# Which gather the GpSimd queue asks for first: late V rows ahead of U rows in a four-layer decoder with product-key experts

## The chip, the core and the metric

One core of a Trainium2 chip runs the whole program as a single launch. The metric is the device time of one execution in microseconds (us). The kernel before was timed three times: 3109.57, 3111.12 and 3113.5 us, median 3111.12 us. One further execution was profiled; views, rows and windows below are of that one.

Engines are called by the profile's names: PE (matmul), DVE (vector), ACT (scalar), POOL (GpSimd), SP (sync).

## The reference, cut to what matters

A residual stream of 256 tokens by 1024 runs through four layers. Each layer is a token mixer (HGRN2, FoX, Mamba-2 SSD, HGRN2 again) and after it a PEER layer: 8 heads pick 16 experts each out of 16384 for every token, so 128 experts a token, and each expert is one row of `u_tab` and one row of `v_tab`, 1024 floats each.

```
def peer_ffn(h, w_q, sub_keys, u_tab, v_tab):
    ...
        idx = jnp.take_along_axis(cand_i, pos, axis=-1)
        gates = jax.nn.softmax(top_s, axis=-1)
        u = jnp.take(u_tab, idx, axis=0)
        v = jnp.take(v_tab, idx, axis=0)
        act = jax.nn.gelu(jnp.einsum('md,mhkd->mhk', xb, u).astype(jnp.float32), approximate=False) * gates
        return jnp.einsum('mhk,mhkd->md', act.astype(xb.dtype), v)
```

The inputs' `norm_ffn` is large, so a good part of the pre-activations is far below zero and their gelu is exactly 0; the V rows of such experts need not be read.

## The kernel before, in words

**Tiling.** A stage is one layer for one block of 128 tokens, so there are eight stages. A stage has 64 steps `i` (8 heads by 8 pairs of ranks); `i` counts on over all stages, 0 to 511. One step handles two gathers `g` = 0 and 1, each of 128 rows: 64 tokens by two ranks, one row per partition. In HBM the U row and the V row of an expert lie side by side in `uv`, 2048 floats.

**What a step does.** `dot(i, g)` on DVE multiplies the gathered U half with the tokens and adds up (one SCALAR_TENSOR_TENSOR of 128x1024, line 219, through a helper). `scaled(i, g)` on ACT takes the gelu. `spread(i)` builds diagonal matrices of the gated activations on ACT and lets PE add the V rows into the stage's sums (`add_rows`, line 1715). Between these, the mixer of the next stage and the routing of coming heads are issued in small portions, so PE, DVE and ACT do both kinds of work in one written order. `ask(i)` on DVE writes an index list for the V rows: a row whose gelu is 0 gets an index beyond the table, and the DMA skips it.

**Three kinds of gather, all issued on POOL's queue in the written order.**
- W (line 1625): a whole row, U and V, 128x2048, 1 MB. It is used for `g` = 0 of even steps.
- U (line 1625): the U half alone, 128x1024, 512 KB. It is used for `g` = 1 of every step but the last few, and also for `g` = 0 of odd steps (where `split(i)` holds).
- V (line 1643, `rest_of`): the V half that belongs to a U. It can be asked for only once `ask(i)` has run, and it skips rows.

Every one of these is one DMA_INDIRECT instruction on POOL, which is busy while it writes the descriptors; the data follow on the DMA engines. Eight completion semaphores go round (DMASW0 to DMASW7), so an issue also waits for the landing of the DMA eight issues earlier.

**Places.** The gathers land in seven buffers of 2048 floats a partition, used as whole places (W) or halves (U, V); `pool[2]` and `pool[1]` are first-in first-out lists of the free ones. `taken` pops the first; `leave` gives it back. A U half goes back when its `dot` is written (`dot`, line 1683), a V half or whole row when its sum is written (`add_rows`, line 1719). The list is filled while the program is built; on the chip the new gather waits for the last reader of its place, which is DVE for a place that a U left and PE for a place that a V or W left.

**Order around the change.** `fetches(n)` is called at the start of step `n`. It asks for the U gather of step n+2 with `g` = 1 (NH = 3), the U or W gather of step n+3 with `g` = 0 (NW = 4), and the V gathers of step n-1: one when n-1 is even, two (`g` = 1, then `g` = 0) when n-1 is odd. Before, the loop put `rest_of(n - 1)` ahead of the first gather with `g` = 0, which comes second in the list; the U gather with `g` = 1 went out ahead of it. The V rows of a step are summed later: `g` = 1 at step i+3 (LAG), `g` = 0 of odd steps at step i+4 (`behind`).

**The bound.** `bounds_check` of a V gather is an integer; each of the 730 calls loads it into a fresh POOL register first.

Of the kernel before, what the change touches and what calls it, by code (L numbers as in the profile page):

```python
# [19 lines left out]
P = 128  # L20
# [3 lines left out]
DEPTH = 4  # L24
# [10 lines left out]
STAGES = 2 * DEPTH  # L35
# [145 lines left out]
def trunk(ctx: ExitStack, tc: tile.TileContext, d: dict, out: bass.AP):  # L181
    nc = tc.nc
# [51 lines left out]
    def C(name):  # L234
        o, n = CONST[name]
        return cst[:, o:o + n]
# [5 lines left out]
    ident, weights = fst[:, 0:P], fst[:, P:]  # L242
    after = C("after")
    tri = C("rb")[:, 0:P]
    small = cpool.tile([P, 2], F32, name="eps")
    eps, spare = small[:, 0:1], small[:, 1:2]
    trimask = cpool.tile([P, P], U8, name="trimask")
# [89 lines left out]
    for l in range(DEPTH):  # L337
        k = KIND[l]
        n = UNITS[UK[k]]
# [16 lines left out]
    for l in range(DEPTH):  # L356
# [9 lines left out]
        for u in ours:  # L366
            t, _, i, where, again = kept[u]
# [1034 lines left out]

    def split(i):

        return i % 2 == 1 and 4 <= i < 64 * (STAGES - 1)

    def apart(i, g=1):

        return g == 1 and i < CLOSE or g == 0 and split(i) or i >= CLOSE + 2

    def route(s, hh):
# [89 lines left out]
        else:  # L1501
# [11 lines left out]
            for o, g, i, j in places:  # L1513
                vec.tensor_copy(gs[o, g], igv[i, :, :, j])
            n = 64 * s + 8 * hh
            halves = ([(gs[:, 0, 0, 1:NQ:2], 0)] if split(n + 1) else []) + [(gs[:, 1, 0], 0)] if n + NQ <= CLOSE else [(gs[:, 1, 0, 0:CLOSE - n], 0), (gs[:, :, 0, CLOSE + 2 - n:], 0)]
            for v, _ in halves:
                vec.tensor_scalar(v, v, 2.0, None, op0=OP.mult)
# [49 lines left out]
    asks = {}  # L1568
# [19 lines left out]
    def taken(n, key):  # L1588

        place[key] = pool[n].pop(0)  # L1590
# [24 lines left out]
    def rows(i, g):  # L1615

        if i >= CLOSE + 2:
            return at_end(4 + 2 * i - 2 * CLOSE + g)
        return place["V", i, g] if apart(i, g) else buffer(i, g)[:, D:]

    def fetch(i, g):
        s, hh, q = pairs[i]
        if i < CLOSE or i < CLOSE + 2 and not g:
            taken(1 if apart(i, g) else 2, ("U" if apart(i, g) else "W", i, g))
        nc.gpsimd.indirect_dma_start(buffer(i, g), None, halved if apart(i, g) else d["uv"],  # L1625
                                     bass.IndirectOffsetOnAxis(ap=got[s, hh][0][:, g, q:q + 1], axis=0))

    def ask(i):

        s, hh, q = pairs[i]  # L1630
        a, n = acts[i], 1 + split(i)
        g = slice(2 - n, 2)
        o = (i // 2 * 3 + i % 2) % 12
        w = index_ring[:, o:o + n]
        vec.tensor_scalar(a[:, g], a[:, 4 - n:4], 0.0, float(FAR), op0=OP.is_equal, op1=OP.mult)
        stt(w, a[:, g], 1.0, got[s, hh][1][:, g, 0, q], op0=OP.add, op1=OP.add)
        asks[i] = [(k, w[:, k + n - 2:k + n - 1]) for k in ((1, 0) if n == 2 else (1,))]

    def rest_of(i):

        for g, w in asks.pop(i):
            taken(1, ("V", i, g))
            nc.gpsimd.indirect_dma_start(rows(i, g), None, halved, bass.IndirectOffsetOnAxis(ap=w, axis=0),  # L1643
                                         bounds_check=2 * DEPTH * P * P - 1, oob_is_err=False)

    def last_rows():

        ix, gs, _ = got[STAGES - 1, 7]
        vec.tensor_scalar(ix[:, :, 0:2], gs[:, :, 0, NQ - 2:], 1.0, None, op0=OP.add)
        for k in range(2):  # L1650
            for g in range(2):
                nc.gpsimd.indirect_dma_start(rows(CLOSE + 2 + k, g), None, halved,
                                             bass.IndirectOffsetOnAxis(ap=ix[:, g, k:k + 1], axis=0))

    def known(i):

        s, hh, _ = pairs[i]
        return got[s, hh][2] if (s, hh) in got else 0

    def fetches(n):  # L1660

        while sent[0] < len(jobs_):
            i, g = jobs_[sent[0]]
            if pairs[i][2] >= known(i) or i >= n + (NH if g else NW) and n < CLOSE - 2:
                break
            if n - 1 in asks and not g:
                rest_of(n - 1)
            if i < CLOSE and not pool[1 if apart(i, g) else 2]:
                break
            fetch(i, g)  # L1670
            sent[0] += 1
        if n - 1 in asks:
            rest_of(n - 1)
        if n == CLOSE:
            last_rows()

# [174 lines left out]
    for s in range(STAGES):  # L1851
# [23 lines left out]
        for i in range(64 * s, 64 * s + 64):  # L1875
            now[0] = i
            if i == 64 * (STAGES - 1) - 3:
                for k in (1, 0):
                    give(2, mix[:, (17 + 2 * k) * D:(19 + 2 * k) * D])
            new, end = i % 64 in TWICE and s > 0, i % 64 == 63 and s + 1 < STAGES  # L1880
            fetches(i)
            dot(i, 0)
            scaled(i, 0)
# [52 lines left out]
```

## Time and profile before

| | |
|---|---|
| median of three runs | 3111.12 us |
| the profiled execution | 3082.27 us |
| its span, first to last instruction | 3080.5 us |
| mean granted PE clock | 0.924 |
| busy PE / DVE / ACT / POOL | 84% / 73% / 48% / 65% |
| moved by DMA | 1221.21 MB, 396 GB/s over the span |
| on POOL's software queue | 1025.36 MB, 83.9% of the time of 16 DMA engines |
| on SP's hardware queue (weights) | 193.55 MB, 15.3% |

The profiled execution is 1.8 us longer than its span and about 29 us (0.9%) shorter than the median of the timed runs. A change that is worked out from the trace is therefore added to the median.

Busy POOL time is time in which it writes descriptors. "Idle before, releaser" in a row is the time in which the engine stood still before that instruction, and what ended it. In a window's row, the last two columns are the mean busy share of the 16 DMA engines (a share a little over 1 comes from packets that overlap) and what they moved.

### The profile page before, as it was taken

Reading aid. Unit: us, or ns where it says so; the run is one execution under the profiler, and the core shown is the slowest. Engines: PE = TensorE matmul, PEld = TensorE weight load, DVE = VectorE, ACT = ScalarE, POOL = GpSimd, SP = SyncE. Lnnn points to the kernel's source line nnn. Section 1 sums busy time; section 2 is a strip of 40 time slices with the busy share of each in tenths; the row PEclk is TensorE's granted clock in tenths of the full one; section 3 lists DMA queues with packets and bytes.
Section 4 is the critical chain, followed back from the end, with each engine's and each line's share of the span. In section 5 each row is a group of like instructions: output and inputs, shape, how many; then the busy total and the mean of one; then the engine's idle time right before and its main releaser. Section 6 shows DMA issues by size and latency. Waiting matters only on the chain.

```text
span 3080.5 us, 36036 instructions
## 1 busy us (share of the span) xinstructions
PE 2585.2 (84%) x9490; PEld 1113.8 (36%) x9490; DVE 2263.0 (73%) x6722; ACT 1470.2 (48%) x4410; POOL 2001.7 (65%) x1766
## 2 busy tenths in 40 slices
PE   9899887988789878999788998889877898976556
PEld 4434343333225424344223543343323253342222
DVE  1687677877877857888687787678768767787764
ACT  2355344464344633687335674355534544443333
POOL 0376576766767766766576655667667676776664
PEclk9999998998899999999889999999988999987887
DMA  7699999999999999999999999999999999999998
GB/s 313 264 396 411 415 405 412 408 413 411 388 404 408 411 404 412 385 414 405 409 384 390 401 413 411 399 400 377 413 410 391 394 412 413 398 392 415 412 414 328
DMA packets 281435, 1221.21 MB, mean 396 GB/s; under 512 B 43099, under 2 KB 43739, under 8 KB 220944
## 3 DMA queue, kind: packets, MB, share of 16 engines
q0 software_dynamic: 253152, 1025.36, 83.9%
q1 hardware_dynamic: 28080, 193.55, 15.3%
q8 instruction: 78, 1.28, 0.2%
q14 instruction: 125, 1.02, 0.1%
HBM read 1266.23 MB, written 1.05 MB: 411 GB/s over the span
## 4 chain that ended last, share of the span: by engine, by line
DMA 43%; PE 23%; DVE 21%; ACT 5%; issue 5%; POOL 2%; POOLq 0%; DVEq 0%; ACTq 0%
DMA arena<-in_uv,ix 25%; DMA arena<-in_uv,ask 17%; DVE arena L219 13%; PE pj L259 11%; PE pj L1715 9%; PE ps L259 3%; ACT L232 2%; DVE cs L219 2%; ACT dots L232 1%; DVE si L219 1%; POOL arena L1625 1%; DVE sv L219 1%; POOL arena L1643 1%; DVE gs L219 1%; ACT arena L232 1%
## 5 line engine op out<-in xcount | busy, mean ns | idle before, releaser
L219 DVE SCALAR_TENSOR_TENSOR arena<-arena 128x1024 f32<-128x1024 f32 (+3 forms) x1282 | 1304.8, 1047 | 430.6 <-DMA arena<-in_uv,ix 409.6
L1625 POOL DMA_INDIRECT arena<-in_uv,ix x1024 | 1144.2, 1117 | 627.9 <-issue 210.0
L1715 PE MATMUL pj<-arena,dh 128*64 128x512 f32 x2048 | 1125.3, 678 | 440.9 <-DMA arena<-in_uv,ask 379.8
L1643 POOL DMA_INDIRECT arena<-in_uv,ask x730 | 848.3, 1162 | 428.5 <-issue 114.6
L1715 PE MATMUL pj<-arena,dg 128*64 128x512 f32 x2048 | 1106.0, 671 | 13.4 <-ACT dg L232 13.1
L232 ACT ACTIVATE dots<-dots 128x1 f32<-128x1 f32 x1024 | 202.6, 200 | 1387.5 <-DVE arena L219 1383.1
L1715 PEld LDWEIGHTS pj<-arena,dh 128*64 128x64 f32 x2048 | 261.0, 148 | 881.4 <-issue 391.7
L259 PE MATMUL pj<-arena 128*128 128x128 f32 (+1 forms) x1752 | 508.9, 439 | 5.4 <-DVE arena L219 4.6
L232 ACT ACT_TABLE_LOAD x332 | 426.0, 1283 | 6.2 <-DVE arena L219 0.8
L259 PE MATMUL pj<-raw,arena 128*128 128x512 f32 x808 | 388.0, 615 | 4.3 <-DVE arena L219 1.9
L1715 PEld LDWEIGHTS pj<-arena,dg 128*64 128x64 f32 x2048 | 265.1, 149 | 343.9 <-issue 235.3
L259 PEld LDWEIGHTS pj<-arena 128*128 128x128 f32 x1752 | 257.6, 191 | 265.4 <-issue 239.5
L259 PEld LDWEIGHTS pj<-raw,arena 128*128 128x128 f32 x808 | 144.8, 193 | 242.5 <-issue 219.2
L232 ACT ACTIVATE dots<-dots,gs 128x1 f32<-128x1 f32 x730 | 187.6, 285 | 9.3
L219 DVE TENSOR_SCALAR dots<-dots 128x1 f32<-128x1 f32 x508 | 82.8, 163 | 122.7 <-ACT dots L232 122.5
L232 ACT ACTIVATE dh<-m,dots 128x64 f32<-128x64 f32 x508 | 168.9, 333 | 4.3 <-PE pj L1715 4.3
L259 PE MATMUL ps<-arena 128*128 128x128 f32 (+6 forms) x1120 | 150.3, 288 | 14.0 <-ACT arena L1223 8.3
L259 PEld LDWEIGHTS ps<-arena 128*128 128x128 f32 (+3 forms) x1120 | 114.5, 171 | 90.4 <-issue 37.3
L232 ACT ACTIVATE dg<-dg,dots 128x64 f32<-128x64 f32 x290 | 100.9, 348 | 9.4
L232 ACT ACTIVATE dg<-m,gs 128x64 f32<-128x64 f32 x290 | 96.4, 332 | 0.0
L219 DVE SCALAR_TENSOR_TENSOR ask<-dots,gs 128x1 int32<-128x1 f32 x508 | 81.7, 161 | 17.5
L219 DVE MAX8 sv<-arena 128x8 f32<-128x128 f32 x256 | 61.3, 281 | 32.2 <-ACT arena L1239 17.3
(131 smaller groups left out, 1875.9 us busy)
## 6 DMA issues: line engine op xcount, KB each, us to landing
raw<-in_ssm SPq DMA_DIRECT2D x48, 1024.0 KB, 8.8
raw<-in_hg SPq DMA_DIRECT2D x35, 1024.0 KB, 9.0
arena<-in_wq SPq DMA_DIRECT2D x28, 1024.0 KB, 8.9
arena<-in_hg SPq DMA_DIRECT2D x27, 1024.0 KB, 13.2
arena<-in_uv,ix POOLq DMA_INDIRECT x1028, 10.7
raw<-in_fox SPq DMA_DIRECT2D x14, 1024.0 KB, 9.2
arena<-in_uv,ask POOLq DMA_INDIRECT x730, 10.2
arena<-in_fox SPq DMA_DIRECT2D x9, 1024.0 KB, 13.9
```

The costliest lines, as they stand in the source:

```text
L219: return getattr(nc.vector, name)(o, *a, **k)
L232: nc.scalar.activation(o, i, f, **k)
L259: nc.tensor.matmul(o, w, m, start=start, stop=stop)
L1625: nc.gpsimd.indirect_dma_start(buffer(i, g), None, halved if apart(i, g) else d["uv"], bass.IndirectOffsetOnAxis(ap=got[s, hh][0][:, g, q: ...
L1643: nc.gpsimd.indirect_dma_start(rows(i, g), None, halved, bass.IndirectOffsetOnAxis(ap=w, axis=0), bounds_check=2 * DEPTH * P * P - 1, oob_ ...
L1715: nc.tensor.matmul(accs[s][e][g * 64:g * 64 + 64], diags[i, g], rows(i, g)[:, e * 512:(e + 1) * 512], start=False, stop=hh == 7 and q == N ...
```

## The change

It makes three edits. `bound` is put into a POOL register once, at the start, and every V gather uses that register. In `split` the condition `i < 64 * (STAGES - 1)` becomes `i // 64 in range(7)`; STAGES is 8, so both hold for the same steps. In `fetches` the V gathers of step n-1 are asked for ahead of the loop, so ahead of the U gather of step n+2 too.

```
+    bound = nc.gpsimd.to_reg(2 * DEPTH * P * P - 1)
...
-        return i % 2 == 1 and 4 <= i < 64 * (STAGES - 1)
+        return i % 2 == 1 and 4 <= i and i // 64 in range(7)
...
             nc.gpsimd.indirect_dma_start(rows(i, g), None, halved, bass.IndirectOffsetOnAxis(ap=w, axis=0),
-                                         bounds_check=2 * DEPTH * P * P - 1, oob_is_err=False)
+                                         bounds_check=bound, oob_is_err=False)
...
     def fetches(n):
 
+        if n - 1 in asks:
+            rest_of(n - 1)
         while sent[0] < len(jobs_):
             i, g = jobs_[sent[0]]
             if pairs[i][2] >= known(i) or i >= n + (NH if g else NW) and n < CLOSE - 2:
                 break
-            if n - 1 in asks and not g:
-                rest_of(n - 1)
             if i < CLOSE and not pool[1 if apart(i, g) else 2]:
                 break
             fetch(i, g)
             sent[0] += 1
-        if n - 1 in asks:
-            rest_of(n - 1)
         if n == CLOSE:
             last_rows()
```

Since both lists of free places are first-in first-out, the V gather now also pops the place that the U gather popped before, and the U gather the next one.

POOL's queue at steps 259 and 260, in the middle of the program, before. "in_uv,ix" marks a U or W gather, "in_uv,ask" a V gather; in brackets are the semaphores that each waits for (DMASW the eight-back landing, DVE a dot or the index list, PE a sum). The first three rows are step 259 (U of 261, V of 258, W of 262), the other four step 260 (U of 262 with `g` = 1, both V of 259, U of 263 with `g` = 0).

```order
L1625 DMA arena<-in_uv,ix 128x1024 [waits DMASW4_49,DVE_49]
L1643 DMA arena<-in_uv,ask 128x1024 [waits DMASW5_49,DVE_49,PE_49]
L1625 DMA arena<-in_uv,ix 128x2048 [waits DMASW6_49,PE_49]
L1625 DMA arena<-in_uv,ix 128x1024 [waits DMASW7_49,PE_49]
L1643 DMA arena<-in_uv,ask 128x1024 [waits DMASW0_49,DVE_49]
L1643 DMA arena<-in_uv,ask 128x1024 [waits DMASW1_49]
L1625 DMA arena<-in_uv,ix 128x1024 [waits DMASW2_49,PE_49]
```

The same seven gathers on POOL's queue after the change, same steps.

```order
L1644 DMA arena<-in_uv,ask 128x1024 [waits DMASW4_49,DVE_49]
L1626 DMA arena<-in_uv,ix 128x1024 [waits DMASW5_49,PE_49]
L1626 DMA arena<-in_uv,ix 128x2048 [waits DMASW6_49,PE_49]
L1644 DMA arena<-in_uv,ask 128x1024 [waits DMASW7_49,DVE_49,PE_49]
L1644 DMA arena<-in_uv,ask 128x1024 [waits DMASW0_49]
L1626 DMA arena<-in_uv,ix 128x1024 [waits DMASW1_49]
L1626 DMA arena<-in_uv,ix 128x1024 [waits DMASW2_49,PE_49]
```

In step 259 the U moved from first to second and its wait turned from DVE to PE; the V lost its wait for PE. In step 260 the U of 262 moved from first to third, behind both V. The W and the last U of a step keep their position, and every position keeps its DMASW semaphore. The first position of a step now always holds a V, which waits for DVE's index list.

POOL's queue at the first step that has a V gather (step 1) and the next, before.

```order
L1625 DMA arena<-in_uv,ix 128x2048 [waits DMAHW7_49]
L1625 DMA arena<-in_uv,ix 128x1024
L1643 DMA arena<-in_uv,ask 128x1024 [waits DMAHW1_49,DMASW0_49,DVE_49]
L1625 DMA arena<-in_uv,ix 128x2048 [waits DMASW1_49,PE_49]
L1625 DMA arena<-in_uv,ix 128x1024 [waits DMASW2_49]
L1643 DMA arena<-in_uv,ask 128x1024 [waits DMASW3_49,DVE_49]
```

The same place after the change.

```order
L1626 DMA arena<-in_uv,ix 128x2048 [waits DMAHW7_49]
L1644 DMA arena<-in_uv,ask 128x1024 [waits DVE_49]
L1626 DMA arena<-in_uv,ix 128x1024 [waits DMAHW1_49,DMASW0_49]
L1626 DMA arena<-in_uv,ix 128x2048 [waits DMASW1_49,PE_49]
L1644 DMA arena<-in_uv,ask 128x1024 [waits DMASW2_49,DVE_49]
L1626 DMA arena<-in_uv,ix 128x1024 [waits DMASW3_49]
```

The U of step 3 stood ahead of the first V and waited for nothing; it now stands behind it. PE, DVE, ACT and SP keep the order of their instructions; only the waits on the landings of the moved gathers go to other semaphores.

More of the change, by code (lines that the diff above doesn't have):

```diff
@@ L244, in trunk @@
     tri = C("rb")[:, 0:P]
+    bound = nc.gpsimd.to_reg(2 * DEPTH * P * P - 1)
     small = cpool.tile([P, 2], F32, name="eps")
@@ L1403, in split @@
     def split(i):
-        return i % 2 == 1 and 4 <= i < 64 * (STAGES - 1)
+        return i % 2 == 1 and 4 <= i and i // 64 in range(7)
     def apart(i, g=1):
@@ L1643, in rest_of @@
             nc.gpsimd.indirect_dma_start(rows(i, g), None, halved, bass.IndirectOffsetOnAxis(ap=w, axis=0),
-                                         bounds_check=2 * DEPTH * P * P - 1, oob_is_err=False)
+                                         bounds_check=bound, oob_is_err=False)
     def last_rows():
@@ L1660, in fetches @@
     def fetches(n):
+        if n - 1 in asks:
+            rest_of(n - 1)
         while sent[0] < len(jobs_):
@@ L1665, in fetches @@
                 break
-            if n - 1 in asks and not g:
-                rest_of(n - 1)
             if i < CLOSE and not pool[1 if apart(i, g) else 2]:
@@ L1671, in fetches @@
             sent[0] += 1
-        if n - 1 in asks:
-            rest_of(n - 1)
         if n == CLOSE:
```

## The prediction

> **What bounds the kernel now.** I read the page's slices first, then the windows, then the chains of waits, then the timeline of one place. The page's span, its DMA slices (40 equal ones of 77 us) and the two groups of gathers on POOL:
>
> ```profile
> span 3080.5 us, 36036 instructions
> ...
> DMA  7699999999999999999999999999999999999998
> GB/s 313 264 396 411 415 405 412 408 413 411 388 404 408 411 404 412 385 414 405 409 384 390 401 413 411 399 400 377 413 410 391 394 412 413 398 392 415 412 414 328
> ...
> L1625 POOL DMA_INDIRECT arena<-in_uv,ix x1024 | 1144.2, 1117 | 627.9 <-issue 210.0
> ...
> L1643 POOL DMA_INDIRECT arena<-in_uv,ask x730 | 848.3, 1162 | 428.5 <-issue 114.6
> ```
>
> The DMA engines are busy nearly throughout, and in most slices they move 404 to 415 GB/s. Where the rate falls, it falls to 377 to 399: that is so in 11 of the 37 slices between the third and the last but one (396, 388, 385, 384, 390, 399, 377, 391, 394, 398, 392). I call these the thin stretches. The windows give the same in us:
>
> ```profile
> 200.00:3000.00 2800.00, 2351.49 (x8698) 1009.26 (x8696) 2119.95 (x6300) 1364.58 (x4128) 1898.21 (x1671) 0.93 1.01 404
> ...
> 300.00:400.00 100.00, 79.06 (x236) 30.27 (x238) 63.99 (x178) 40.25 (x118) 54.84 (x49) 0.86 1.02 413
> ...
> 800.00:900.00 100.00, 79.75 (x281) 30.53 (x280) 79.29 (x231) 45.45 (x148) 78.81 (x69) 0.91 1.00 391
> ...
> 1600.00:1700.00 100.00, 87.71 (x341) 37.62 (x341) 77.41 (x230) 52.02 (x155) 69.25 (x60) 0.92 1.00 389
> ```
>
> The columns are PE, PEld, DVE, ACT and POOL busy with their counts, the granted clock, the DMA share and GB/s. A full window moves 413 GB/s at share 1.02. From 200 to 3000 us the mean is 404, so 2800 x (1 - 404/413) = 61 us is all that a better order of the same bytes could win there. The change moves no bytes. The Trainium skill has another ceiling: "DMA: Bandwidth & Descriptors", section Specifications, gives a core about 358 GB/s from HBM; by it the kernel would already be over its bound and no order could win anything. The trace disagrees with 413 GB/s in a window, so the ceiling here is the row's.
>
> What makes a stretch thin? In 800:900 POOL writes descriptors for 78.81 us in 69 gathers, and the timeline below shows 0.30 us idle ahead of each even when nothing is waited for: 78.81 + 69 x 0.30 = 99.5 of 100 us. There the issuing itself is the bound. In 300:400 it is 54.84 + 49 x 0.30 = 69.5, and POOL waits for landings. So the kernel alternates: full stretches, where DMA paces everything, and thin ones, where POOL issues back to back or waits for DVE or PE. The waits, first of DVE and PE for gathers, then of POOL:
>
> ```profile
> DVE arena L219 <- DMA arena<-in_uv,ix: 409.6, 237, 6.8
> PE pj L1715 <- DMA arena<-in_uv,ask: 379.8, 172, 8.7
> ```
> ```profile
> POOL arena L1625 <- DMA arena<-in_uv,ix: 153.1, 154, 3.8
> ...
> POOL arena L1643 <- DMA arena<-in_uv,ix: 106.7, 92, 3.1
> POOL arena L1643 <- DMA arena<-in_uv,ask: 54.1, 117, 2.3
> POOL arena L1643 <- PE pj L1715: 52.9, 57, 2.8
> POOL arena L1625 <- PE pj L1715: 31.0, 61, 2.7
> ...
> POOL arena L1643 <- DVE ask L219: 17.4, 13, 3.5
> ...
> POOL arena L1643 <- DVE arena L219: 14.2, 15, 2.1
> ...
> POOL arena L1643 <- DVE si L219: 8.6, 14, 2.6
> ...
> POOL arena L1643 <- DVE cs L219: 8.1, 14, 1.8
> POOL arena L1643 <- DVE sv L219: 7.9, 8, 4.3
> ```
>
> Columns: us in total, times, longest. DVE waits for U about as long as PE waits for V, so neither kind of gather is plainly the later one. A V waits for DVE (the last five rows: 13 + 15 + 14 + 14 + 8 = 64 times, 56.2 us) in about one of eight of the 508 steps that have a V; in the rest the index list is there before POOL comes to it.
>
> **The bound in a register.** What goes is one register move for each V:
>
> ```profile
> L1643 POOLq MOVE  x730: 29/29/35, 115.5 to 3050.6; - x183
> ...
> DMA to landing us min/median/max: 5.7/10.2/25.5
> ```
>
> 730 x 29 ns = 21 us, if they stood on POOL's path. They do not: POOL's sequencer runs them ahead, under the descriptor writing of the gather before, and the idle time is 0.30 us ahead of a V (which has a MOVE) and of a U (which has none) alike, rows below. So 0, with 21 us as the end of what it could win if that cover were gone, and nothing that it could lose but one move at the start.
>
> **The condition in `split`.** It holds for the same steps; 0, without a range.
>
> **V first.** One place shows it, steps 259 and 260. POOL first (W of 262, U of 262, both V of 259, U of 263), then DVE: the dot of (259, 1), the index list, the two dots of step 260, and the dot of (262, 1).
>
> ```profile
> 1630.58 1.53 POOL L1625 DMA_INDIRECT arena<-in_uv,ix  x1 [0.59 <-PE pj L1715]
> 1632.42 0.94 POOL L1625 DMA_INDIRECT arena<-in_uv,ix  x1 [0.30 <-PE pj L1715]
> 1634.78 1.74 POOL L1643 DMA_INDIRECT arena<-in_uv,ask  x1 [1.42 <-DVE ask L219]
> 1636.82 1.56 POOL L1643 DMA_INDIRECT arena<-in_uv,ask  x1 [0.31 <-issue]
> 1638.69 1.12 POOL L1625 DMA_INDIRECT arena<-in_uv,ix  x1 [0.30 <-PE pj L1715]
> ```
> ```profile
> 1632.65 1.22 DVE L219 SCALAR_TENSOR_TENSOR arena<-arena 128x1024 f32<-128x1024 f32 x1
> ...
> 1634.35 0.16 DVE L219 SCALAR_TENSOR_TENSOR ask<-dots,gs 128x2 int32<-128x2 f32 x1
> 1634.43 1.22 DVE L219 SCALAR_TENSOR_TENSOR arena<-arena 128x1024 f32<-128x1024 f32 x1
> ...
> 1636.29 1.22 DVE L219 SCALAR_TENSOR_TENSOR arena<-arena 128x1024 f32<-128x1024 f32 x1
> ...
> 1645.29 1.23 DVE L219 SCALAR_TENSOR_TENSOR arena<-arena 128x1024 f32<-128x1024 f32 x1
> ```
>
> Before, the U of 262 went out at 1632.42, while the index list was still being made, and the V at 1634.78 right behind the list. After, POOL stands from 1632.11 (1630.58 + 1.53) to 1634.78, issues the two V at 1634.78 and 1636.82 as now, then the U of 262 at 1638.69 instead of 1632.42, and the U of 263 at about 1640.1, one issue (1.12 + 0.30) late. Here, then, the V win nothing, the U of 262 comes 6.27 us later, and POOL loses 1.42 us. Queued behind the waiting V on POOL are the step's U and W; who waits for them is DVE, at their dots. The dot of (262, 1) began at 1645.29. With the median way from issue to landing of a U, 10.7 us (below), a U issued at 1638.69 lands at 1649.4, 4.1 us behind that; in this stretch the queue is short, and with the shortest way, 5.5 us, it would be 1.1 us ahead.
>
> ```profile
> DMA to landing us min/median/max: 5.5/10.7/27.2
> ```
>
> Where the list is ready in time (seven of eight steps), the swap is plain. A V goes out one issue earlier, 1.12 + 0.30 = 1.42 us (a U's mean and the gap), and a U one or two V issues later: 1.16 + 0.30 = 1.46 us in odd steps, 2.92 us in even ones. PE gets V earlier, DVE gets U later. The V with `g` = 0 is summed four steps after its own, the U it now overtakes is needed two steps later: the order puts the less urgent ahead.
>
> Now what reaches the end. In a full stretch nothing does: 26 of 37 slices move all that DMA moves, and what waits for what there only hands DMA's pace on. The room under it is kept as long as POOL still issues ahead: from a U's issue to the index list it leads to lie 10.7 us to landing and 1634.35 + 0.16 - 1632.65 = 1.9 us from dot to list, 12.6; the U of step n+2 goes out in step n and its list is wanted at the head of step n+3, three steps of 3080.5/512 = 6.0 us less 2.9 us, 15.1. So 2.5 us remain.
>
> In the thin stretches, 11/37 of the program, I count both sides. Loss: 64 late lists x 11/37 = 19 places, each with up to one issue of idle POOL, 1.42 us: 27 us at most, 0 at least, since the queue still holds gathers then. Gain: POOL's waits for PE's sums, 52.9 + 31.0 = 83.9 us, x 11/37 = 25 us at most, if the earlier V made every such sum come in time; 0 at least, where PE is late from its mixers' matmuls. The later U cost DVE nothing while their landing keeps ahead of the dots, and by the example about as much as POOL loses where it does not. I take about half of each, +15 and -12: a loss late lists cause is nearest the example, where POOL did lose its 1.42 us but the queue was not yet empty; and a sum that POOL waits for waited for a V in some cases only (172 of PE's waits in 512 steps). Sum of the parts: 0 + 0 + 15 - 12 = +3 us, on a profiled execution of 3082.27 us, 0.1%. On the median of the timed runs, 3111.12, that is **3114 us**.
>
> **Beside it, the port.** A V's issue takes 1.00 us in the median (row below); in the rows above those under a dot take 1.74 (from 1634.78, the dot from 1634.43) and 1.56 us. The issues now start right behind the index list, so more of them fall under the dots of the step that follows. The Trainium skill says this of the two engines: "SBUF — State Buffer", section Who interferes with whom, that a DVE instruction with two SBUF inputs contends with a GpSimd instruction that reads SBUF. By that rule the trace's 1.74 is the price of a dot, and the trace agrees.
>
> ```profile
> L1643 POOL DMA_INDIRECT arena<-in_uv,ask x730: 993/1000/2086, 124.4 to 3052.5; - x183
> ```
>
> Priced from these rows: 19 places x (1.74 - 1.00) for each of two V is 28 us of POOL at most. In the back-to-back stretch (800:900) it is 0: the issues already run under every dot. I take 0 and keep the rest as a rival.
>
> **The rivals.**
> - *The lists hold up POOL* (slower). Mechanism: the first gather of each step waits for `ask`, the U behind it lands later, its dot is later, and so is the list after it. The point from which it decides: when the way from a U's issue to its landing goes over 10.7 + 2.5 = 13.2 us, or the dot comes 2.5 us late for other reasons, the loop closes and runs from stall to stall. For it: DVE already waits 237 times for U. Against it: a held-up POOL makes the queue, and so that way, shorter. Price: the 27 us without the 12: 3111 + 27 = 3138 us. Chance 0.24.
> - *The port* (slower): half of the 28 us, added to the +3: 3128 us. Chance 0.08.
> - *V were the late ones* (faster): POOL's waits for sums go and the lists cost nothing, -25 us: 3086 us. For it: PE's 379.8 us; against it: only what lies in thin stretches counts, and DVE's 409.6 us get longer. Chance 0.23.
> - *It does nothing* (no change): the moves were hidden, the condition is the same, and the swap is covered by the full queue at both kinds of stretch: 3111 us. Chance 0.10.
>
> **How the numbers follow.** The forecast, losses and gains that nearly cancel, has 0.35, its own range is +-6 us. A measurement of this kernel (3109.57 to 3113.5 in three runs) can tell about 0.2%, 6 us, from no change. Within that: 0.35 + 0.10 = 0.45; slower 0.24 + 0.08 = 0.32; faster 0.23. The range goes from half-way into the faster rival (3111 - 19 = 3092) to the slower rival's 3138.
>
> **What would show it.** Right: the row "L1643 <- DVE ask" and its kin grow from 56 us, "L1643 <- PE pj L1715" goes to near 0 and turns up at the U's line, DVE's 409.6 us grow and PE's 379.8 shrink, and the mean of 200:3000 stays at 403 to 405 GB/s. Wrong towards slower: fewer slices over 404, the medians from issue to landing (V 10.2, U 10.7 us) fall under 9.5 us and POOL's idle time is put down to DVE. Wrong towards faster: the thin slices rise over 400 with POOL's waits for PE gone. A gap under 0.30 us ahead of a V would show that the moves did stand on the path.

## The result and the profile after

The changed kernel takes 3133.01 us in the median of ten runs (3122.43 to 3140.48) where the kernel before, beside it, takes 3114.32: 1.0057 of before, 95% interval 1.004 to 1.0074. One of the ten runs of before, 3514.03 us, lies far above all others and is not in that ratio. The changed kernel is slower, by 18.7 us. The profiled execution after takes 3128.17 us, near its median; that of before, 3082.27 us, was quicker than every run of before in this comparison (the lowest is 3108.71), so the two traces lie 46 us apart, of which the change can be blamed for less than half. I take sizes from the timed ratios, and from the traces which waits came and went. Two traces of one later comparison, `bound_only` (the order of before) and `swap_only` (the order of the change), serve beside them; both are described below.

The page of the changed kernel, span and DMA slices first, then the two groups of gathers (count, busy us, mean ns, idle us ahead of them):

```profile
span 3126.4 us, 35394 instructions
...
GB/s 309 252 402 397 414 396 407 399 404 411 376 391 408 399 410 411 385 413 395 412 376 389 386 409 409 394 394 372 413 405 381 364 387 414 395 377 414 414 408 333
...
L1626 POOL DMA_INDIRECT arena<-in_uv,ix x1024 | 1151.8, 1125 | 557.2 <-issue 259.2
...
L1644 POOL DMA_INDIRECT arena<-in_uv,ask x730 | 877.5, 1202 | 508.2 <-DVE ask L219 163.4
```

Of the 37 slices between the third and the last but one, 19 lie under 400 GB/s; before it was 11. In the pair of one comparison it is 14 in `swap_only` and 9 in `bound_only`. The fullest slices are as full as they were (414). The same windows after (PE, PEld, DVE, ACT, POOL busy; clock; DMA share; GB/s):

```profile
200.00:3000.00 2800.00, 2350.45 (x8634) 978.49 (x8630) 2082.18 (x6228) 1348.13 (x4069) 1906.48 (x1644) 0.94 1.01 398
300.00:400.00 100.00, 77.09 (x242) 29.95 (x241) 62.32 (x174) 36.65 (x109) 54.30 (x47) 0.91 1.02 414
800.00:900.00 100.00, 70.68 (x248) 26.25 (x248) 78.15 (x238) 39.05 (x138) 77.67 (x67) 0.90 0.98 374
```

From 200 to 3000 us the DMA moves 398 GB/s, not 404; 2800 x (1 - 398/404) = 42 of the 46 us between the spans lie there. The pair of one comparison, `bound_only` and then `swap_only`, shows the same with 405 and 400:

```profile
200.00:3000.00 2800.00, 2339.36 (x8711) 1005.27 (x8711) 2124.54 (x6308) 1367.63 (x4138) 1904.39 (x1676) 0.94 1.01 405
```
```profile
200.00:3000.00 2800.00, 2361.19 (x8657) 979.80 (x8656) 2096.46 (x6264) 1353.18 (x4092) 1915.85 (x1653) 0.94 1.01 400
```

The window 300:400 is untouched. 800:900, where POOL already issued back to back, falls from 391 to 374 GB/s, with 67 gathers issued instead of 69. What POOL waits for now (us in total, times, longest):

```profile
POOL arena L1644 <- DVE ask L219: 163.4, 99, 5.4
...
POOL arena L1644 <- DMA arena<-in_uv,ix: 55.3, 44, 3.7
POOL arena L1626 <- PE pj L1714: 55.0, 80, 3.3
POOL arena L1626 <- DMA arena<-in_uv,ask: 45.7, 54, 3.0
POOL arena L1626 <- DMA arena<-in_uv,ix: 44.5, 79, 2.9
...
POOL arena L1644 <- DVE sv L219: 21.1, 18, 5.7
...
POOL arena L1644 <- DVE gt L219: 13.9, 11, 2.4
POOL arena L1644 <- DVE cs L219: 13.0, 17, 2.5
POOL arena L1644 <- DVE ts L219: 11.3, 13, 2.4
```

The five largest rows of a V that waits for DVE come to 222.7 us in 158 waits; before the five largest were 56.2 us in 64. All such rows together come to 280.4 us in 232 waits; before, 81.6 in 101. In exchange POOL stands less for landings: 352 us, all rows of a wait for a DMA, in `bound_only`, 201 in `swap_only`. (The trace after lacks a part of the landings, so I compare these two.) So in many steps POOL is held up by the index list, where before it more often stood because the queue was full. DVE's and PE's waits for gathers, and two more of PE's:

```profile
DVE arena L219 <- DMA arena<-in_uv,ix: 423.1, 254, 9.8
```
```profile
PE pj L1714 <- DMA arena<-in_uv,ask: 211.0, 92, 10.1
PE pj L1714 <- ACT dg L232: 84.1, 65, 5.8
PE pj L1714 <- ACT dh L232: 40.6, 19, 4.1
```

Those two in the kernel before:

```profile
PE pj L1715 <- ACT dh L232: 34.6, 12, 6.0
PE pj L1715 <- ACT dg L232: 15.6, 17, 2.2
```

PE's wait for V falls from 379.8 to 211.0 us: V do come earlier. But PE needs more than the V for a sum: `dg` and `dh` are the diagonals that ACT makes, and their gelu needs the dot of the U. PE's waits for them grow from 50 to 125 us, and all of PE's waits together stay where they were: 487 us before and 506 after, 500 in `bound_only` and 489 in `swap_only`. One wait took the place of the other.

The same place as in the prediction, steps 259 and 260, on POOL (V of 258, U of 261, W of 262; both V of 259, U of 262, U of 263):

```profile
1648.31 1.00 POOL L1644 DMA_INDIRECT arena<-in_uv,ask  x1 [0.30 <-issue]
1649.61 0.94 POOL L1626 DMA_INDIRECT arena<-in_uv,ix  x1 [0.30 <-issue]
1650.85 1.85 POOL L1626 DMA_INDIRECT arena<-in_uv,ix  x1 [0.30 <-DVE ix L219]
1655.47 1.22 POOL L1644 DMA_INDIRECT arena<-in_uv,ask  x1 [2.77 <-issue]
1657.00 1.57 POOL L1644 DMA_INDIRECT arena<-in_uv,ask  x1 [0.30 <-issue]
1658.87 1.11 POOL L1626 DMA_INDIRECT arena<-in_uv,ix  x1 [0.30 <-issue]
1660.29 0.95 POOL L1626 DMA_INDIRECT arena<-in_uv,ix  x1 [0.30 <-PE ps L264]
```

And on DVE there: the dot of (259, 1), the list of step 259, the dot of (260, 0):

```profile
1652.83 1.22 DVE L219 SCALAR_TENSOR_TENSOR arena<-arena 128x1024 f32<-128x1024 f32 x1
...
1654.53 0.16 DVE L219 SCALAR_TENSOR_TENSOR ask<-dots,gs 128x2 int32<-128x2 f32 x1
1654.61 1.22 DVE L219 SCALAR_TENSOR_TENSOR arena<-arena 128x1024 f32<-128x1024 f32 x1
```

POOL is free at 1652.70 and stands 2.77 us at the V, with the U of 262 queued behind it; the list is written at 1654.69; the U, which before went out first, goes out at 1658.87. The row calls the end of that wait "issue" (no release that the profile shows). The list accounts for the wait up to 1654.69; before, the V went out 0.27 us behind its list, here 0.78, and what fills the other half microsecond the trace does not show. As before, a dot starts right behind the list, and the issue of the V falls under it: it takes 1.22 us, the next 1.57.

### The profile page after: what moved, and what is told of

Its sections match the earlier page's. It is cut to its first block, busy times and chain, and to the rows that moved or that the text cites. A ratio compares the mean times of both kernels' runs of the same rounds, so it can differ in the third digit from the quotient of the medians.

```text
span 3126.4 us, 35394 instructions
## 1 busy us (share of the span) xinstructions
PE 2612.6 (84%) x9490; PEld 1089.9 (35%) x9490; DVE 2255.7 (72%) x6722; ACT 1468.7 (47%) x4410; POOL 2038.5 (65%) x1766
## 4 chain that ended last, share of the span: by engine, by line
DMA 35%; PE 24%; DVE 15%; issue 11%; POOL 7%; ACT 5%; another core or an unknown queue 2%; POOLq 0%; DVEq 0%; SPq 0%; ACTq 0%
DMA arena<-in_uv,ix 25%; PE pj L260 11%; DVE arena L219 10%; DMA arena<-in_uv,ask 9%; PE pj L1714 9%; POOL arena L1626 4%; PE ps L260 4%; POOL arena L1644 3%; ACT L232 2%; DVE cs L219 1%; ACT dots L232 1%; ACT arena L232 1%; PE ps L264 1%; DVE gs L219 1%
## 5 line engine op out<-in xcount | busy, mean ns | idle before, releaser
L219 DVE SCALAR_TENSOR_TENSOR arena<-arena 128x1024 f32<-128x1024 f32 (+3 forms) x1282 | 1306.6, 1047 | 484.2 <-DMA arena<-in_uv,ix 423.1
L1714 PE MATMUL pj<-arena,dh 128*64 128x512 f32 x2048 | 1083.5, 656 | 274.8 <-DMA arena<-in_uv,ask 211.0
L1644 POOL DMA_INDIRECT arena<-in_uv,ask x730 | 877.5, 1202 | 508.2 <-DVE ask L219 163.4
L1714 PE MATMUL pj<-arena,dg 128*64 128x512 f32 x2048 | 1063.9, 647 | 90.7 <-ACT dg L232 83.9
L1714 PEld LDWEIGHTS pj<-arena,dh 128*64 128x64 f32 x2048 | 254.0, 144 | 638.2 <-issue 418.5
L1714 PEld LDWEIGHTS pj<-arena,dg 128*64 128x64 f32 x2048 | 256.9, 145 | 544.6 <-issue 298.9
L264 PE MATMUL ps<-fst,arena 128*128 128x128 f32 x504 | 77.7, 280 | 33.7 <-DVE arena L219 15.7
L219 DVE SCALAR_TENSOR_TENSOR ask<-dots,gs 128x1 int32<-128x1 f32 x508 | 81.6, 161 | 17.5
```

The lines of the kernel that those rows point to most:

```text
L219: return getattr(nc.vector, name)(o, *a, **k)
L264: nc.tensor.transpose(o, i, ident)
L1714: nc.tensor.matmul(accs[s][e][g * 64:g * 64 + 64], diags[i, g], rows(i, g)[:, e * 512:(e + 1) * 512], start=False, stop=hh == 7 and q == N ...
```

## The experiments

The kernel before was run beside each group: 3079.20 us for the first four kernels (`swap_only`, `bound_only`, `places_old`, `places_new`), 3078.84 for the second four (`after_again`, `swap_one`, `swap_two`, `after_list_early`), 3110.66 for the last four (`blank_op`, `list_gate`, `v0_last`, `u_first`). Each group ran on another chip. Each ratio is to its own before.

**The swap alone, and the register alone.** First the swap without the register.

```
-    bound = nc.gpsimd.to_reg(2 * DEPTH * P * P - 1)
...
-                                         bounds_check=bound, oob_is_err=False)
+                                         bounds_check=2 * DEPTH * P * P - 1, oob_is_err=False)
```

> V gathers ahead of the U gather as in the changed kernel, in the places of the changed kernel, but the bound loaded at every V gather as before. Theory (the index list holds up POOL at the head of a step): 1.0057 of before, like the changed kernel, +18 us, between 1.004 and 1.0075; the row of POOL's V waiting for DVE's list (163 us in the changed kernel, 17 before) stays over 120 us. Rival (the register costs or saves something): off the changed kernel's ratio by more than 0.002.

Measured: 3106.12 us, 1.0087 (1.007 to 1.0105), and V waits 160.3 us for the list. That is above the theory's range and 0.003 off the first 1.0057, as the rival would have it; but the two ratios are of different comparisons. So I ran the changed kernel again in the second group, whose kernel before was as quick as that of the first:

> The changed kernel as it is, beside the others on one chip. Its ratio was 1.0057 on one chip, and its order without the register 1.0087 on another. Every theory: between 1.004 and 1.0105; it is the mark for the other three.

Measured: 3106.74 us, 1.0089 (1.0074 to 1.0104). With and without the register is the same, so the loss is the swap's, all of it. The rewritten condition stands in both; it was not tried alone, but it holds for the same steps, and the engines' instruction counts are the same before and after (9490 on PE, 6722 on DVE, 4410 on ACT, 1766 on POOL). The size of the loss differs by occasion: 0.4 to 0.7% in one comparison, 0.7 to 1.0% in the others.

The register without the swap, in the kernel before (`bound_only`):

```
+    bound = nc.gpsimd.to_reg(2 * DEPTH * P * P - 1)
...
-                                         bounds_check=2 * DEPTH * P * P - 1, oob_is_err=False)
+                                         bounds_check=bound, oob_is_err=False)
```

> The old order and the old places, with the bound in one register. Theory: the moves ran under the descriptor writing, so 1.000 of before, within 0.002; POOL's gap ahead of a V stays 0.30 us. Rival (the moves stood on the path): up to 730 x 0.029 = 21 us faster, 0.993. Rival (reading a long-lived register costs): slower by up to what the changed kernel lost, 1.0057.

Measured: 3078.13 us, 1.0002 (0.9992 to 1.0013). Theory holds, both rivals fall. Its POOL rows show the gap ahead of a U and of a V without a MOVE, 0.30 us as before:

```profile
1002.05 0.94 POOL L1626 DMA_INDIRECT arena<-in_uv,ix  x1 [0.30 <-issue]
...
1008.59 1.00 POOL L1644 DMA_INDIRECT arena<-in_uv,ask  x1 [0.30 <-issue]
```

Since it is the old order at a usual speed, it is also a second trace of before: span 3074.0 us.

**Position or place.** The swap changes two things at once: the position on POOL's queue and which place a gather takes. One kernel keeps the new positions with the old places (a later line that would break off for want of a place is changed to match and not shown):

```
+            if ("U", i, g) not in place:
+                taken(1 if apart(i, g) else 2, ("U" if apart(i, g) else "W", i, g))
...
     def fetches(n):
 
+        if sent[0] < len(jobs_) and jobs_[sent[0]][1]:
+            i = jobs_[sent[0]][0]
+            if i < CLOSE and pairs[i][2] < known(i) and i < n + NH and pool[1]:
+                taken(1, ("U", i, 1))
         if n - 1 in asks:
             rest_of(n - 1)
```

> The issue order of the changed kernel, but every gather in the place that it has before (the U is given its place first, then V ahead of it on the queue). Theory (what costs is the position on the queue: POOL stands for the list, and the U lands later): 1.004 to 1.008, at least as slow as the changed kernel, with over 120 us of V waiting for DVE. Rival (what costs is that the U now waits for a place that PE has to sum): under 1.002, since the U again takes a place that a dot has left.

Measured: 3116.70 us, 1.0115 (1.0098 to 1.0132). The other keeps the old positions with the new places, taken ahead of the loop:

```
-            taken(1, ("V", i, g))
...
     def fetches(n):
 
+        for g, _ in asks.get(n - 1, ()):
+            taken(1, ("V", n - 1, g))
         while sent[0] < len(jobs_):
```

> The issue order of before, but every gather in the place that the changed kernel gives it: the U at the head of a step waits for PE's sum, the V behind it takes the place that a U left. Theory (position on the queue): 1.000 to 1.002; the list is there when POOL comes to the V. Rival (the place): 1.004 or more, with POOL's U waiting for PE well over the 31 us of before.

Measured: 3091.71 us, 1.0039 (1.0022 to 1.0056). The first fits the theory in its sign and in V's waits for DVE (213 us, all rows), but lies above its range of 1.004 to 1.008; there the V at the head of a step also stands for PE's sums (73 us, all rows; before, 72). The second does not fit, and the rival's reading does: the place costs too, if the U stays first, since the U then waits for PE's sum at the head of the step. The row of U waiting for PE went from 31.0 us in 61 waits to

```profile
POOL arena L1626 <- PE pj L1717: 158.3, 151, 7.1
```

So the position with the old places costs 1.15%, and the new places take a part of that back (to 0.87% in the same comparison; the two intervals still touch). Neither half of the change is good by itself. A reading that fits both is that the U goes out later, once for the list and the V, once for PE.

**How far the U moves.** V ahead of U only where a step has one V, and only where it has two.

```
     def fetches(n):
 
+        if n % 2 and n - 1 in asks:
+            rest_of(n - 1)
```

(and `n % 2 == 0` in the other).

> V ahead of U only in the steps that have one V (the U comes one V later); in the steps with two V the order of before. Bound in a register. Theory (the loop from a U's issue over its dot and the list to the next head of a step gets too short; the cost grows with how far the U is moved back): the smaller part, 1.001 to 1.003. Rival (POOL merely stands for a late list at the head of a step, once a step whatever follows): half of the loss, like the other half, 1.003 to 1.005.

> V ahead of U only in the steps that have two V (the U comes two V later); in the steps with one V the order of before. Bound in a register. Theory (cost grows with how far the U is moved back): the larger part, 1.004 to 1.007. Rival (late list at the head, once a step): like the other half, 1.003 to 1.005.

Measured: 3093.34 us, 1.0043 (1.003 to 1.0055), and 3105.09 us, 1.008 (1.0067 to 1.0094). The further the U goes back, the more it costs, as the theory had it, though both parts are a little over its ranges (the smaller one lies in the rival's). The rival's equal halves fall. Distance is not all that differs: V's waits for DVE come to 146 us where the steps with one V are swapped, and to 195 where those with two are. Together the two parts would give 1.23%, and the whole swap gives 0.89%, so they do not add up; why is not shown.

**The list a little earlier.** In the changed kernel, `ask(i)` put ahead of the mixer's portion on DVE.

```
-            d0 = dve[0]
-            others()
             if i < CLOSE:
                 ask(i)
+            d0 = dve[0]
+            others()
```

> The changed kernel with one step moved: the index list is written right after the diagonals of its step, ahead of the mixer's portion on DVE instead of behind it. Theory (POOL stands for the list): V waiting for DVE falls from 279 us in all to under 220, and the time comes back by a part, 1.001 to 1.005. Rival (the list is not what counts, only the U that lands later): as the changed kernel, within 0.002 of it.

Measured: 3130.26 us, 1.0168 (1.0146 to 1.019). It was to give time back and cost more instead: a miss. DVE's own row gives the likely reason. The list needs the gelu from ACT, and the mixer's portion used to lie under that wait:

```profile
DVE dots L219 <- ACT dots L232: 202.1, 501, 4.5
```

In the changed kernel run beside it:

```profile
DVE dots L219 <- ACT dots L232: 115.7, 345, 3.3
```

With 86 us more of idle DVE the lists came no earlier on the whole: V's waits for DVE, all rows together, are 308 us, against 291 there. The experiment did not shorten the way to the list, so it does not test the theory; it suggests that DVE's time in that loop is dear too.

**POOL stands, but no V overtakes.** The order of before, and a small POOL copy that reads the list ahead of each step's first gather; the control copies a constant.

```
+            if n - 1 in asks:
+                nc.gpsimd.tensor_copy(seen[:, 0:1], asks[n - 1][0][1])
```

(in the control the source is `seen[:, 1:2]`; `seen` is two more columns of the tile that holds the lists.)

> The control for list_gate: the same POOL copy at the same place, from a constant instead of the list, so that it waits for nothing. It prices the instruction alone: 508 times some 0.1 us and a gap of 0.3 us, 200 us of POOL's time, of which only what lies in thin stretches can count: 1.000 to 1.006 by every theory.

> Order and places of before (U first, then V), bound in a register, and one small POOL copy of one column of the index list ahead of each step's first gather: POOL stands for the list at the head of the step, but no V overtakes a U. Theory A (standing for the list is what costs): at least 0.004 above blank_op, near the changed kernel's 1.0089. Theory B (the U's later place behind one or two V is what costs, as swap_two over swap_one suggests): within 0.002 of blank_op.

Measured: the control 3140.83 us, 1.0096 (1.0074 to 1.0117), the gate 3154.25 us, 1.0143 (1.0124 to 1.0161). The copies' rows, of the gate and of the control:

```profile
L1665 POOL COPY ask<-ask 128x1 int32<-128x1 int32 x508 | 192.2, 378 | 74.0 <-DVE ask L219 65.8 <-DVE sf L219 2.1 <-DVE dots L219 1.1
```
```profile
L1666 POOL COPY ask<-ask 128x1 int32<-128x1 int32 x508 | 184.1, 362 | 2.9
```

The control is dear, above the range that was set for it: a copy takes 0.362 us, not 0.1, and 508 x (0.362 + 0.30) = 336 us of POOL's time make the run 30 us longer, about 9% of it. Standing for the list comes on top: 1.0143/1.0096 = 1.0047. This is nearer theory A (0.004 or more) than B (under 0.002), but it is not sharp. The intervals are near +-0.002, and the control's six runs fall into four at 3134 to 3142 us and two at 3153 to 3154, as slow as the gate's; both profiled executions take 3153 us, so the two traces show no difference in time at all. And the gate's copies stand for 74 us in all, where V stands for DVE for 280 us in the changed kernel. So it is likely, not shown, that POOL's stand for the list is a part of the loss even with no V ahead of the U.

**The other way.** The second V of a step behind the step's last U:

```
-                rest_of(n - 1)
+                rest_of(n - 1, 1)
...
+        todo = asks.pop(i)
+        if todo[most:]:
+            asks[i] = todo[most:]
+        for g, w in todo[:most]:
```

> The other way from the change: order of before, but in the steps with two V the second V (summed four steps later) goes behind the step's last U instead of ahead of it. Bound in a register. Theory (what counts is how soon U lands and its list is made): no slower, 0.997 to 1.001. Rival (late V are what PE and the places wait for): 1.002 or more.

Measured: 3106.10 us, 0.9994 (0.998 to 1.0007): no change. And every U and W of a step ahead of every V (the two lines that put V ahead inside the loop are left out):

> Every U and whole row of a step ahead of every V of that step, the furthest from the change. Bound in a register. Theory (only U's lateness counts): within 0.003 of before. Rival (V are as urgent; the order of before is between two cliffs): 1.003 or more, with PE's wait for V well over the 380 us of before.

Measured: 3126.30 us, 1.0052 (1.0032 to 1.0071). The rival holds as to the time, not as to its sign: PE's wait for V did not grow (328.2 us in 160 waits). The row that grew is again one of POOL's, now of U that wait for the sums that free a place, ahead of the V queued behind:

```profile
POOL arena L1626 <- PE pj L1714: 109.7, 79, 7.8
```

In the kernel before that row was 31.0 us. So moving V ahead of U costs, moving all V behind costs too, and only the second V had room.

## Why the prediction was half right

The forecast was 3114 us, no change that could be told apart. What came is a loss of 18.7 us, 0.6%, and 0.9% in two later comparisons: a slower kernel, outside the forecast's own +-6 us. That 3133 us lies inside the stated range is luck of its width: the range was drawn up to the slower rival's 3138 us, and down to 3092, which is three quarters of the way to the faster rival and not half.

**What bounds the kernel**: as far as the traces show, right. Full stretches did not change (413 and 414 GB/s in 300:400), and there are more thin ones.

**The register and the condition at 0**: right, by `bound_only` (1.0002) and by `swap_only` and `after_again` (1.0087 and 1.0089) for the register; the condition was not tried alone.

**V first, +15 - 12 = +3**: this is the step that failed. The kinds of wait were right, both sizes were not.

The gain of 12 us did not come. It was half of what POOL's waits for PE's sums could give back. These waits moved from V's line to U's and did not shrink: 112.5 us in `bound_only`, all rows, 113.8 in `swap_only`. (In the traces before and after they are 118.7 and 90.9.) PE's waits for V fell by 169 us, and PE waited for the diagonals behind the U instead.

The loss of 15 us was counted with "64 late lists", which are V's waits for DVE at the V's old place on the queue. The change puts the V at the head of the step, where POOL comes earlier, and there more lists are late. The timeline of before tells how many, from the end of each `ask` on DVE and the end of POOL's gather before: of 508 lists, 27 were written after POOL came free for their V, by 33 us in all, but 112 were written after POOL came free at the head of their step, ahead of the U, by 143 us. In the changed kernel 166 lists are written after POOL comes free for their V, by 208 us. In the pair of one comparison the same three counts are 26 and 94 in `bound_only` and 161 in `swap_only` (34, 121 and 191 us). So the larger part of the growth could be counted in the trace of before, at the right place. The rest, 54 lists in the one case and 67 in the other, comes on top. A loop would do that: a later U makes its dot later, the dot its list, and the list the next U. That this loop is what adds them is argued, not shown. "11/37 of the program", held fixed, also grew: 9 to 14 thin slices in the pair.

**The room of 2.5 us** in that loop was worked out from medians (and the 10.7 us is of a line that holds U and W together); half of all ways are longer. The deciding point was a way of 13.2 us from issue to landing, or a dot 2.5 us late for other reasons. The first did not come. The way got shorter instead, though not under the 9.5 us that were named as a sign of a slower kernel. The U's line, `swap_only` and then `bound_only`:

```profile
DMA to landing us min/median/max: 5.1/10.0/25.1
```
```profile
DMA to landing us min/median/max: 6.3/10.7/23.8
```

The U still came later for DVE, since they went out later: DVE waits for them for 466.8 us in `swap_only`, 426.9 in `bound_only`. With POOL at 86% of its time before (1898 us of issuing and 1671 gaps of 0.30, in 2800), a stand of 1 to 3 us leaves little room to catch up before the next step, 6 us later; that, too, is argued.

**The rivals.** "The lists hold up POOL" is nearest to what came: +27 us was its price, against +18.7 here and about +27 in the two later comparisons; I had given it 0.24, and no change 0.45. The experiments bear it out in part: the cost grows when the U moves further back (`swap_one`, `swap_two`), a smaller cost appears when the U waits for PE instead (`places_new`), and one may appear with no V ahead (`list_gate` over `blank_op`, not sharp). "The port" left a trace of its size: a V's issue takes 1202 ns, not 1162, x 730 = 29 us of POOL, where 28 was priced at most. It goes with the dots: of the 730 issues of a V in `bound_only`, the 480 that overlap a dot take 1.24 us in the mean and the others 1.01; in `swap_only` 518 overlap one. By the control's 9% the 29 us would be some 3 us of the run, an estimate. "V were the late ones" falls: V came earlier, and PE's and POOL's waits only changed their names.

**The signs I named**: V's waits for DVE grew, its waits for PE went to near 0 and turned up at U's line, DVE's wait grew (409.6 to 423.1) and PE's shrank, as for the forecast; the mean of 200:3000 at 398 instead of 403 to 405, and 17 slices of 404 GB/s or more instead of 24, are what I had named for slower, as is POOL's idle time put down to DVE. The medians under 9.5 us did not come.

What stays open: how much of the 0.6 to 0.9% is POOL's stand and how much the V ahead of the U. A kernel with the list ready early and no DVE time spent on it would tell; it was not tried. Nor was the port tried alone.

## What to carry to other kernels

On a queue that issues in order, the wait of the first request is a wait of all behind it. Here it was better to let the U, whose index was ready and whose landing starts the way to the next list, go ahead of a V that waits for a fresh list. It is no rule without an end: with every U and W ahead of every V the kernel was slower too (`u_first`, 1.0052), and U stood 110 us for sums that free their places, not 31.

Count late events at the place to which a change moves the request, not at the place where it stands now: 112 lists were late at the head of the step, 27 at the V. And do not hold such counts fixed across the change.

A wait that shrinks (here PE's for V, by 169 us) is no gain if the same work then waits for something else. Look at the sum of an engine's waits.

## What the runs showed of the hardware

A POOL copy of one number a partition costs 362 ns and a gap of 0.30 us, and 508 of them made this run 30 us longer, more than the change under study. An index list written at 1634.51 us released POOL's next issue 0.27 us later. The kernel before ran at 3114, 3079, 3079 and 3111 us in the four comparisons, up to 1.1% apart, more than the effect itself; only ratios within one comparison can be read, and even these gave 1.0057 and 1.0089 for the same kernel.
